# Forward substitution of a gated-DeltaNet kernel in its own lane, three rows in two steps

## The chip, the cores and the metric

The kernel runs on one core of one Trainium2 chip, in one launch. The metric is device time in microseconds (us), the median of three runs. The kernel before takes 1953.09 us (1953.03 to 1953.24). TensorE (PE) does the matmuls, VectorE (DVE) and ScalarE (ACT) work element by element, GpSimd (POOL) does a few selects and powers, and SyncE (SP) issues most DMAs. Each engine takes its instructions strictly in the order in which they stand in its own queue.

## The reference

One decoder block of width 2048 on 256 tokens, in float32: a half-step SwiGLU feed-forward, a mixer, a second feed-forward, a gated embedding, and a norm. The change is in the mixer, which projects the normed input by `W_in` into 14 blocks of 512 columns, runs a gated DeltaNet on 8 heads and a stick-breaking attention on 8 other heads, and projects both by `W_out`:

```
lmat = where(strict, einsum("bnhid,bnhjd->bnhij", k_beta, k) * decay, 0)     # 64 x 64 per chunk and head
sol  = triangular_solve(lmat + eye, rhs, lower, unit_diagonal)               # forward substitution
step: v_new = u - w S;  o = (q e^g) S + attn v_new;  S = S e^g_last + (k e^..)^T v_new
```

## The kernel before

**Steps.** Every large product is a loop over weight pairs. `accumulate` (L107 to L109) handles one pair of 256 weight rows by 512 columns in 12 matmuls of 512 columns. Float32 accuracy comes from splitting: `weight_pair` loads `raw` (SP, L69), casts it to `whi` on ACT (L72) and subtracts to get `wlo` on DVE (L73). PE uses `whi` in the first matmul of a pair and `wlo` in the second or third. I call one pair a step and number the steps of the mixer from 0: steps 0 to 111 are the 14 blocks of `W_in`, steps 112 to 143 are `W_out`. There are three buffers of `whi` and of `wlo`, so the split of pair n can start when step n-3 has ended.

**Lanes.** Beside the steps run generators in lanes. After each step `lanes.step()` advances the generator at the head of every lane to its next `yield`. So what a generator issues between two yields is spread over the steps. Lane CONV does the short convolutions, SYSTEM builds the triangular systems of a group of four heads (`system`, L940), CHAIN solves them and runs the recurrence (`chain`, L996), STICK runs the attention heads (`stick`).

**The solve.** The eight 128 x 128 systems of a head group (four heads, two halves of the tokens) are cut into 32 x 32 diagonal blocks, and all are inverted at once, row by row, for i from 1 to 31. Row i is one product (L1007, `pm`, 8(i+1) elements in each partition) and one reduction over it (L1009, into `sol`), both on DVE, and each needs the one before. Then `sol` goes to DRAM (L1013) and comes back turned into `Z` (L1017), DVE transposes three blocks of it into `X` (L1021 to L1023), and four small products join the blocks: t1 (L1029), z1 (L1037), t2 (L1047), z2 (L1053). Between them stand copies out of PSUM on ACT and DVE: `ts`, `X`, `Z`, `tw`. The recurrence follows: up, sp, op, ks, qs, vp, op (L1060), with `R` and others on DVE. `L`, the table of factors, has one buffer; the second group's `system` loads it (L988) once the first group's solve is done.

**Order.** The generators only fix in which order the instructions are recorded. A scheduler then orders each engine's queue by its own estimates, so a recorded instruction can go earlier than others that were recorded before it, if its inputs come earlier. `tc.keep_in_program_order` pins an instruction behind everything recorded so far on its engine.

Of the kernel before, what the change touches and what calls it, by code (L numbers as in the profile page):

```python
# [13 lines left out]
ALU = mybir.AluOpType  # L14
AX = mybir.AxisListType

P = 128
# [24 lines left out]
def block_kernel(ctx, tc, a, out):  # L42
    nc = tc.nc
# [11 lines left out]
    def mx_ps(name):  # L55
        return ps.tile([P, NB], F32, tag="mx", name=name, bufs=4)

    lanes = Lanes(4)
    dr = ctx.enter_context(tc.tile_pool(name="dr", bufs=1, space=bass.MemoryType.DRAM))


# [532 lines left out]
    def r1():  # L594
# [8 lines left out]

    stat = new_stat()
    nT = mixer(tc, nc, a, act, mm_ps, mx_ps, accumulate, picker, new_nT, norm_block, sumsq, block, lanes, transposed,
               nT, r, h, stat, ident, mhalf)
    r = rstd(stat)
# [94 lines left out]
def mixer(tc, nc, a, act, mm_ps, mx_ps, accumulate, picker, new_nT, norm_block, sumsq, block, lanes, transposed,  # L702
          nT, r, h, stat, ident, mhalf):
    xs = picker(*nT)
    C64 = P // 2
    CONV, CHAIN, STICK, SYSTEM = 0, 1, 2, 3
    blocks = list(W_IN_ORDER)

    with tc.tile_pool(name="mix", bufs=1) as mp, \
# [49 lines left out]
        def transpose4(name, src):  # L759
            tr = mx_ps(name)  # L760
            for c in range(4):
                nc.tensor.transpose(tr[:, c * P:(c + 1) * P], src(c), ident)
            return tr

        def bc(x):

            return x.rearrange("p (c o) -> p c o", o=1).broadcast_to([P, 4, P])

        def v3(x):
            return x.rearrange("p (c e) -> p c e", c=4)  # L770
# [4 lines left out]
        def w4(name, dt=F32):  # L775
            return mp.tile([P, 4 * T], dt, tag="w4", name=name, bufs=6)
# [87 lines left out]
        knq = [[mp.tile([P, 4, 2, P], F32, tag="kq", name="knq", bufs=4) for _ in range(2)] for _ in range(2)]  # L864
        kdec = [mp.tile([P, NB], F32, tag="kd", name="kdec", bufs=2) for _ in range(2)]
        vn_ = [w4("v").rearrange("p (t x) -> p t x", t=2) for _ in range(2)]
# [65 lines left out]
        def dn_block(part, hg):  # L932
            nat = to_sbuf(natural(2 * part + hg))
            lanes.add(CONV, conv_silu(nat, part, hg))


        o_nat = [mp.tile([P, 2, NB], F32, tag="onat", name="onat", bufs=2) for _ in range(2)]
# [3 lines left out]
        def system(hg):  # L941

            hs = slice(hg * 4, hg * 4 + 4)
            kq = knq[hg]
            while not decayed:
                yield

            dec = w4("dec").rearrange("p (t c i) -> p t c i", t=2, c=4)
            for t in range(2):
                gb = transpose4("gb", lambda c: gc[:, t, hg * 4 + c:hg * 4 + c + 1].broadcast_to([P, P]))  # L950
                for b, s in ((0, gc), (C64, sB)):
                    nc.vector.tensor_tensor(out=dec[:, t, :, b:b + C64], in0=v3(gb)[:, :, b:b + C64],
                                            in1=bc(s[:, t, hs])[:, :, 0:C64], op=ALU.subtract)
                nc.gpsimd.affine_select(out=dec[:, t], in_=dec[:, t], pattern=[[0, 4], [1, P]],
                                        compare_op=ALU.is_ge, fill=-1e30, base=0, channel_multiplier=-1)
                nc.scalar.activation(dec[:, t], dec[:, t], AF.Exp)
            yield
            yield
            while ready[hg] < 3:
                yield  # L960

            nc.vector.tensor_tensor(out=v3(kdec[hg]), in0=v3(kdec[hg]), in1=bc(eT[:, 0, hs]), op=ALU.mult)

            AT = w4("AT").rearrange("p (t c i) -> p t c i", t=2, c=4)
            for t in range(2):
                for pr in range(2):
                    kk = mx_ps("kk").rearrange("p (c w i) -> p c w i", c=2, w=2)
                    for q in range(2):
                        c = 2 * pr + q
                        nc.tensor.matmul(kk[:, q], kq[t][:, c, 0, :], kq[t][:, c], start=True, stop=True)  # L970
                    nc.vector.tensor_tensor(out=AT[:, t, 2 * pr:2 * pr + 2], in0=kk[:, :, 1, :],
                                            in1=dec[:, t, 2 * pr:2 * pr + 2], op=ALU.mult)
                    for q in range(2):
                        c = 2 * pr + q
                        nc.vector.scalar_tensor_tensor(out=dec[:, t, c], in0=kk[:, q, 0, :],
                                                       scalar=nbeta[:, t, hg * 4 + c:hg * 4 + c + 1], in1=dec[:, t, c],
                                                       op0=ALU.mult, op1=ALU.mult)
                yield
            N = dec.rearrange("p t c i -> p (t c) i")

            sc = dp.tile([H, 4, 32, 32], F32, tag="sc", name="sc", bufs=2)
            for b in range(4):
                nc.sync.dma_start(out=sc[:, b].rearrange("x j i -> j x i"),
                                  in_=N[32 * b:32 * b + 32, :, 32 * b:32 * b + 32])
            while hg and not solved[0]:
                yield
            L = mp.tile([P, 4 * T], F32, tag="lt", name="L")
            nc.sync.dma_start(out=L, in_=sc.rearrange("x b j i -> (x b) (j i)")  # L988
                              .rearrange("q (o n) -> q o n", o=1).broadcast_to([32, 4, 1024]))
            sol = mp.tile([P, 8, 32], F32, tag="sol", name="sol")  # L990
            nc.sync.dma_start(out=sol, in_=a["eye32"].rearrange("(o g) n -> o g n", o=1).broadcast_to([32, 4, 256]))
            for _ in range(5):
                yield
            systems[hg] = AT, N, L, sol

        def chain(hg):  # L996
            hs = slice(hg * 4, hg * 4 + 4)
            kq, v, o = knq[hg], vn_[hg], o_nat[hg]
            while hg not in systems:
                yield  # L1000
            AT, N, L, sol = systems[hg]

            nc.vector.memset(L[:, 0:1024:33], 1.0)
            Lv = L.rearrange("p (j i) -> p i j", j=32)
            for i in range(1, 32):
                pm = mp.tile([P, 8, 32], F32, tag="pm", name="pm")
                nc.vector.tensor_tensor(out=pm[:, :, 0:i + 1], in0=sol[:, :, 0:i + 1],  # L1007
                                        in1=Lv[:, i:i + 1, 0:i + 1].broadcast_to([P, 8, i + 1]), op=ALU.mult)
                nc.vector.tensor_reduce(out=sol[:, :, i:i + 1], in_=pm[:, :, 0:i + 1], axis=AX.X, op=ALU.add)  # L1009
                if i % 2:  # L1010
                    yield
            sc2 = dp.tile([H, 4, 32, 32], F32, tag="sc2", name="sc2", bufs=2)
            nc.sync.dma_start(out=sc2.rearrange("x b (g c) i -> (x b g) (c i)", g=4),  # L1013
                              in_=sol.rearrange("p c i -> p (c i)"))
            solved[hg] = True
            for b in range(4):
                nc.sync.dma_start(out=Z[32 * b:32 * b + 32, :, 32 * b:32 * b + 32],  # L1017
                                  in_=sc2[:, b].rearrange("x m i -> m x i"))
# [166 lines left out]
        def stick():  # L1185
            while not chain_done[0] or 1 not in systems:
                yield
            for part in range(2):
                sbT[part].append(mp.tile([P, 4, T], F32R, tag="kq", name="sbT", bufs=4))
            for part in range(2):  # L1190
                sbT[part].append(w4("sbT", F32R).rearrange("p (c x) -> p c x", c=4))
            live = {}
            for i in range(H + 3):
                if i >= 3:
                    stick_c(i - 3, live.pop(i - 3))
                if 2 <= i <= H + 1:
                    stick_b(live[i - 2])
                if i < H:
                    while sb_ready[i // 4] < 3:
                        yield  # L1200
                    live[i] = stick_a(i)
                yield
# [27 lines left out]
        for hg in range(2):  # L1230
            for part in (1, 0, 2):
                dn_block(part, hg)
            lanes.add(SYSTEM, system(hg))
            lanes.add(CHAIN, chain(hg))
        lanes.add(STICK, stick())
        for hg in range(2):
# [91 lines left out]
```

## Time and profile before

| | |
|---|---|
| median of three runs | 1953.09 us |
| profiled execution, its own time | 1952.66 us |
| its span, first to last instruction | 1950.9 us |
| busy in the span | PE 99%, DVE 82%, ACT 60%, POOL 7% |
| granted TensorE clock | 0.999 |

The mixer's steps 0 to 111 lie between 695 and 1068 us of the span. A step without anything else takes PE 2.72 us (12 matmuls, 0.227 us from one start to the next). The listed length of one matmul, 0.39 us, overlaps the next, so the distance of starts tells where PE lost time, and a bracket at a row's end tells the idle time before it and who ended it.

### The profile page before, as it was taken

Reading aid. Unit: us, or ns where it says so; the run is one execution under the profiler, and the core shown is the slowest. Engines: PE = TensorE matmul, PEld = TensorE weight load, DVE = VectorE, ACT = ScalarE, POOL = GpSimd, SP = SyncE. Lnnn points to the kernel's source line nnn. Section 1 sums busy time; section 2 is a strip of 40 time slices with the busy share of each in tenths; the row PEclk is TensorE's granted clock in tenths of the full one; section 3 lists DMA queues with packets and bytes.
Section 4 is the critical chain, followed back from the end, with each engine's and each line's share of the span. In section 5 each row is a group of like instructions: output and inputs, shape, how many; then the busy total and the mean of one; then the engine's idle time right before and its main releaser. Section 6 shows DMA issues by size and latency. Waiting matters only on the chain.

```text
span 1950.9 us, 24300 instructions
## 1 busy us (share of the span) xinstructions
PE 1930.9 (99%) x8888; PEld 1594.4 (82%) x8888; DVE 1591.7 (82%) x1737; ACT 1161.9 (60%) x1364; POOL 143.9 (7%) x220
## 2 busy tenths in 40 slices
PE   9999999999999999999999999999999999999998
PEld 7888888888888888878788888888888888888887
DVE  7879988998889766797856579889888998889765
ACT  7655666566665567664555456566565655656554
POOL 0010100000010000010100000010000100000000
PEclk9999999999999999999999999999999999999999
DMA  8778888888888765556564786788898987988764
GB/s 310 273 213 293 252 290 278 244 288 250 267 284 253 223 218 165 172 171 215 167 206 158 243 284 234 225 270 285 256 283 249 319 254 239 274 254 258 244 213 142
DMA packets 143895, 474.01 MB, mean 243 GB/s; under 512 B 19616, under 2 KB 47264, under 8 KB 129568
## 3 DMA queue, kind: packets, MB, share of 16 engines
q1 hardware_dynamic: 106048, 296.92, 43.7%
q0 software_dynamic: 25056, 157.30, 29.3%
q10 hardware_dynamic: 12672, 18.25, 3.1%
q8 instruction: 69, 1.13, 0.2%
q14 instruction: 50, 0.41, 0.1%
HBM read 450.39 MB, written 22.02 MB: 242 GB/s over the span
## 4 chain that ended last, share of the span: by engine, by line
PE 83%; DVE 9%; issue 5%; DMA 1%; ACT 1%; POOL 0%; SPq 0%; POOLq 0%; DVEq 0%; ACTq 0%
PE d L516 5%; PE d L518 5%; PE d L517 5%; PE u L517 5%; PE u L518 4%; PE u L516 4%; PE g L517 3%; PE g L518 3%; PE g L516 3%; PE g L326 3%; PE g L327 3%; PE g L325 3%; PE pj L108 3%; PE pj L109 3%; PE pj L107 3%
## 5 line engine op out<-in xcount | busy, mean ns | idle before, releaser
L72 ACT CAST whi<-raw 128x1024 fp32r<-128x1024 f32 (+1 forms) x493 | 515.8, 1050 | 424.1 <-PE pj L109 106.4
L73 DVE TENSOR_TENSOR wlo<-raw,whi 128x1024 fp32r<-128x1024 f32 (+1 forms) x493 | 595.9, 1216 | 160.9 <-ACT whi L72 160.0
L291 DVE TENSOR_TENSOR slo<-R,shi 128x2048 fp32r<-128x2048 f32 (+2 forms) x217 | 435.9, 2013 | 103.0 <-ACT shi L290 102.3
L290 ACT CAST shi<-R 128x2048 fp32r<-128x2048 f32 (+2 forms) x217 | 366.3, 1692 | 190.7 <-DVE R L295 76.4
L107 PE MATMUL pj<-whi,nTh 128*128 128x512 f32 x448 | 179.4, 401 | 0.0
L108 PE MATMUL pj<-wlo,nTh 128*128 128x512 f32 x448 | 175.4, 391 | 2.2 <-DVE wlo L73 2.2
L109 PE MATMUL pj<-whi,nTl 128*128 128x512 f32 x448 | 174.9, 390 | 0.0
L517 PE MATMUL d<-wlo,hTh 128*128 128x512 f32 x448 | 174.3, 389 | 0.0
L518 PE MATMUL d<-whi,hTl 128*128 128x512 f32 x448 | 174.0, 389 | 0.0
L516 PE MATMUL d<-whi,hTh 128*128 128x512 f32 x448 | 173.6, 390 | 0.0
L517 PE MATMUL u<-wlo,nTh 128*128 128x512 f32 x400 | 156.2, 390 | 3.4 <-DVE wlo L73 3.4
L517 PE MATMUL g<-wlo,nTh 128*128 128x512 f32 x400 | 156.0, 390 | 1.0 <-DVE wlo L73 1.0
L518 PE MATMUL g<-whi,nTl 128*128 128x512 f32 x400 | 155.9, 390 | 0.0
L518 PE MATMUL u<-whi,nTl 128*128 128x512 f32 x400 | 155.7, 389 | 0.0
L516 PE MATMUL g<-whi,nTh 128*128 128x512 f32 x400 | 155.1, 391 | 0.2 <-ACT whi L72 0.2
L516 PE MATMUL u<-whi,nTh 128*128 128x512 f32 x400 | 153.7, 389 | 0.0
L295 DVE TENSOR_TENSOR R<-R 128x2048 f32<-128x2048 f32 (+2 forms) x66 | 133.1, 2016 | 0.1
L108 PEld LDWEIGHTS pj<-wlo,nTh 128*128 128x128 f32 x448 | 84.2, 188 | 20.1 <-DVE wlo L73 4.1
L516 PEld LDWEIGHTS d<-whi,hTh 128*128 128x128 f32 x448 | 84.1, 188 | 17.9 <-ACT hTh L479 0.7
L518 PEld LDWEIGHTS d<-whi,hTl 128*128 128x128 f32 x448 | 84.1, 188 | 17.7
L109 PEld LDWEIGHTS pj<-whi,nTl 128*128 128x128 f32 x448 | 84.1, 188 | 17.6
L517 PEld LDWEIGHTS d<-wlo,hTh 128*128 128x128 f32 x448 | 84.1, 188 | 17.5
(311 smaller groups left out, 3472.8 us busy)
## 6 DMA issues: line engine op xcount, KB each, us to landing
raw<-in_w_gu SPq DMA_DIRECT2D x199, 512.0 KB, 5.7
raw<-in_w_down SPq DMA_DIRECT2D x112, 512.0 KB, 6.3
raw<-in_w_in SPq DMA_DIRECT2D x112, 512.0 KB, 3.4
R<-in_w_gu2q POOLq DMA_DIRECT2D x54, 1024.0 KB, 8.2
R<-in_w_gu1q POOLq DMA_DIRECT2D x48, 1024.0 KB, 8.5
raw<-in_w_out SPq DMA_DIRECT2D x32, 512.0 KB, 4.0
raw<-in_w_pg SPq DMA_DIRECT2D x32, 512.0 KB, 4.3
R<-in_w_down11q POOLq DMA_DIRECT2D x12, 768.0 KB, 6.2
```

The source lines that it names most:

```text
L72: nc.scalar.copy(hi[:, j, :], raw[:, j, :])
L73: nc.vector.tensor_tensor(out=lo[:, j, :], in0=raw[:, j, :], in1=hi[:, j, :], op=ALU.subtract)
L107: nc.tensor.matmul(outs[t], xh[:, c], whi[:, j, :], start=st, stop=False)
L108: nc.tensor.matmul(outs[t], xh[:, c], wlo[:, j, :], start=False, stop=False)
L109: nc.tensor.matmul(outs[t], xl[:, c], whi[:, j, :], start=False, stop=sp)
L290: nc.scalar.copy(hi, w)
L291: nc.vector.tensor_tensor(out=lo, in0=w, in1=hi, op=ALU.subtract)
L295: nc.vector.tensor_tensor(out=self.raw[x], in0=self.raw[x], in1=self.raw[y], op=ALU.add)
L325: nc.tensor.matmul(out, xh, whi[:, g, :], start=st, stop=False, skip_group_check=True)
L516: nc.tensor.matmul(out, xh[:, c], whi[:, j, :], start=st, stop=False, skip_group_check=True)
L517: nc.tensor.matmul(out, xh[:, c], wlo[:, j, :], start=False, stop=False, skip_group_check=True)
L518: nc.tensor.matmul(out, xl[:, c], whi[:, j, :], start=False, stop=sp, skip_group_check=True)
```

## The change

The loop over the rows is taken out of `chain` and becomes a generator of its own, `solve`, in a fifth lane, SOLVE. `chain` now waits until `solve` has stored its solution, and begins with the load of `Z`. So the solve of the second group no longer stands behind the recurrence of the first in one lane. A generator that yielded after every second row (`if i % 2`) now yields after two rows out of three (`if i % 3`). And the product of each row is pinned behind what was recorded for DVE before it.

```diff
-    lanes = Lanes(4)
+    lanes = Lanes(5)
...
-    CONV, CHAIN, STICK, SYSTEM = 0, 1, 2, 3
+    CONV, CHAIN, STICK, SYSTEM, SOLVE = range(5)
...
-        def chain(hg):
-            hs = slice(hg * 4, hg * 4 + 4)
-            kq, v, o = knq[hg], vn_[hg], o_nat[hg]
+        solutions = {}
+
+        def solve(hg):
             while hg not in systems:
                 yield
             AT, N, L, sol = systems[hg]
...
             for i in range(1, 32):
                 pm = mp.tile([P, 8, 32], F32, tag="pm", name="pm")
-                nc.vector.tensor_tensor(out=pm[:, :, 0:i + 1], in0=sol[:, :, 0:i + 1],
-                                        in1=Lv[:, i:i + 1, 0:i + 1].broadcast_to([P, 8, i + 1]), op=ALU.mult)
+                tc.keep_in_program_order(
+                    nc.vector.tensor_tensor(out=pm[:, :, 0:i + 1], in0=sol[:, :, 0:i + 1],
+                                            in1=Lv[:, i:i + 1, 0:i + 1].broadcast_to([P, 8, i + 1]), op=ALU.mult))
                 nc.vector.tensor_reduce(out=sol[:, :, i:i + 1], in_=pm[:, :, 0:i + 1], axis=AX.X, op=ALU.add)
-                if i % 2:
+                if i % 3:
                     yield
...
             solved[hg] = True
+            solutions[hg] = AT, N, sc2
+
+        def chain(hg):
+            hs = slice(hg * 4, hg * 4 + 4)
+            kq, v, o = knq[hg], vn_[hg], o_nat[hg]
+            while hg not in solutions:
+                yield
+            AT, N, sc2 = solutions[hg]
             for b in range(4):
...
             lanes.add(SYSTEM, system(hg))
+            lanes.add(SOLVE, solve(hg))
             lanes.add(CHAIN, chain(hg))
```

The rows below show what stands in the engines' queues. Of a product of eight elements in a row, `128x8x28` is row 27. The changed kernel's line numbers are 4 to 13 higher from L999 on.

ACT around the first head group's joining products, before (z1 stands before step 65 on PE, and the first cast after `ts` is that of step 66):

```order
L746 ACTIVATE nat<-pj,rstd_5474 128x512 x2
L1032 COPY ts<-t_7420 32x8x32
L72 CAST whi<-raw 128x1024 x2
L1040 COPY X<-z_7470 32x8x32
L1042 COPY Z<-z_7470 32x8x32
L72 CAST whi<-raw 128x1024 x2
L1054 COPY Z<-z_7551 64x8x64
```

Two casts stood between `ts` and `X`. The same place on ACT now (the casts ahead of `ts` end with that of step 69; the one behind `Z` is that of step 70):

```order
L746 ACTIVATE nat<-pj,rstd_5474 128x512 x2
L72 CAST whi<-raw 128x1024 x4
L1044 COPY ts<-t_7535 32x8x32
L1052 COPY X<-z_7579 32x8x32
L1054 COPY Z<-z_7579 32x8x32
L72 CAST whi<-raw 128x1024 x2
L1066 COPY Z<-z_7663 64x8x64
```

`X` and `Z` now follow `ts` at once, and four casts have gone ahead of all three. On PE now, from the end of z1 to the start of step 70 (before, the 12 matmuls of a step stood between z1, t2 and z2):

```order
L1051 MATMUL z_7579<-Z,ts 32x32
L1059 MATMUL t_7628<-X,dec 64x64 x8
L1065 MATMUL z_7663<-Z,tw 64x64 x7
L107 MATMUL pj<-whi,nTh 128x512 x2
L1065 MATMUL z_7663<-Z,tw 64x64
L108 MATMUL pj<-wlo,nTh 128x512
```

The three products now stand next to each other, just ahead of step 70.

DVE at that place, before (the `wlo` above `Z` is that of step 67):

```order
L73 TENSOR_TENSOR wlo<-raw,whi 128x1024
L1041 COPY Z<-z_7470 32x8x32
L1009 TENSOR_REDUCE sol<-pm 128x8
L1007 TENSOR_TENSOR pm<-sol,L 128x8x7
L1009 TENSOR_REDUCE sol<-pm 128x8
L1007 TENSOR_TENSOR pm<-sol,L 128x8x8
L1009 TENSOR_REDUCE sol<-pm 128x8
L1007 TENSOR_TENSOR pm<-sol,L 128x8x9
L1049 COPY tw<-t_7518 64x512
L1009 TENSOR_REDUCE sol<-pm 128x8
L73 TENSOR_TENSOR wlo<-raw,whi 128x1024
```

Eight instructions of rows and both copies stood between `wlo` 67 and `wlo` 68, and t1 to z2 lay three steps apart. Now (the first `wlo` is that of step 70):

```order
L1053 COPY Z<-z_7579 32x8x32
L1011 TENSOR_TENSOR pm<-sol,L 128x8x6
L1061 COPY tw<-t_7628 64x512
L1013 TENSOR_REDUCE sol<-pm 128x8
L1011 TENSOR_TENSOR pm<-sol,L 128x8x7
L1013 TENSOR_REDUCE sol<-pm 128x8
L1011 TENSOR_TENSOR pm<-sol,L 128x8x8
L73 TENSOR_TENSOR wlo<-raw,whi 128x1024
L1013 TENSOR_REDUCE sol<-pm 128x8
L73 TENSOR_TENSOR wlo<-raw,whi 128x1024 x3
```

Both copies now stand between `wlo` 69 and `wlo` 70, with two rows between `tw` and `wlo` 70.

DVE from `wlo` 80 on, before (the second group's solve ended ahead of `wlo` 75):

```order
L1183 TENSOR_TENSOR sbT<-so,sbT 128x256
L73 TENSOR_TENSOR wlo<-raw,whi 128x1024
L167 STREAM_TRANSPOSE tb<-nat 128x512 x2
L73 TENSOR_TENSOR wlo<-raw,whi 128x1024 x8
L167 STREAM_TRANSPOSE tb<-nat 128x512 x2
```

No row of a solve stood here. Now, from `wlo` 85 on (`wlo` 86 is the second):

```order
L73 TENSOR_TENSOR wlo<-raw,whi 128x1024
L1195 TENSOR_TENSOR sbT<-so,sbT 128x256
L1011 TENSOR_TENSOR pm<-sol,L 128x8x25
L1013 TENSOR_REDUCE sol<-pm 128x8
L1011 TENSOR_TENSOR pm<-sol,L 128x8x26
L1013 TENSOR_REDUCE sol<-pm 128x8
L1011 TENSOR_TENSOR pm<-sol,L 128x8x27
L1013 TENSOR_REDUCE sol<-pm 128x8
L73 TENSOR_TENSOR wlo<-raw,whi 128x1024
L1011 TENSOR_TENSOR pm<-sol,L 128x8x28
L1013 TENSOR_REDUCE sol<-pm 128x8
```

The second group's longest rows moved from steps 70 to 75 to steps 81 to 89. Over all, the first group's solve stands between `wlo` 39 and `wlo` 64 (before: 39 to 54) and the second's between `wlo` 66 and `wlo` 89 (before: 65 to 75). The order of all engines before step 40 and from step 112 on is the same as before.

## Rows read from the trace of the kernel before

**Rows 1.** Who PE waited for: total us, times, longest.
```profile
PE pj L108 <- DVE wlo L73: 2.2, 4, 1.1
PE vp L1060 <- DVE R L1081: 1.3, 1, 1.3
...
PE at L1172 <- DVE st L1165: 0.6, 1, 0.6
```

**Rows 2.** Stretches: length, PE, PEld, DVE, ACT, POOL busy, PE clock, DMA share, GB/s.
```profile
818.00:868.50 50.50, 49.37 (x239) 40.16 (x238) 46.66 (x101) 31.81 (x66) 5.86 (x4) 1.00 0.47 160
901.00:941.00 40.00, 38.74 (x282) 32.35 (x275) 38.16 (x87) 18.93 (x36) 0.53 (x1) 1.00 0.48 159
960.00:1060.00 100.00, 100.00 (x582) 83.98 (x581) 56.32 (x73) 52.89 (x84) 4.62 (x9) 1.00 0.59 190
```

**Rows 3.** PE in order of time: two waits, first matmuls of steps 76 and 80.
```profile
844.96 0.39 PE L107 MATMUL pj<-whi,nTh 128*128 128x512 f32 x1
845.65 0.50 PE L108 MATMUL pj<-wlo,nTh 128*128 128x512 f32 x1 [0.30 <-DVE wlo L73]
...
928.14 0.39 PE L109 MATMUL pj<-whi,nTl 128*128 128x512 f32 x1
929.79 1.13 PE L1060 MATMUL vp<-R,Z 128*128 128x128 f32 x8 [1.26 <-DVE R L1081]
...
948.51 0.58 PE L107 MATMUL pj<-whi,nTh 128*128 128x512 f32 x1
...
962.27 0.39 PE L107 MATMUL pj<-whi,nTh 128*128 128x512 f32 x1
```

**Rows 4.** A step without other work: DVE splits pair 93, PE uses it.
```profile
993.48 1.22 DVE L73 TENSOR_TENSOR wlo<-raw,whi 128x1024 fp32r<-128x1024 f32 x1 [1.50 <-ACT whi L72]
...
997.86 0.39 PE L108 MATMUL pj<-wlo,nTh 128*128 128x512 f32 x1
```

**Rows 5.** DVE in order of time around `tw`.
```profile
907.38 0.18 DVE L1009 TENSOR_REDUCE sol<-pm 128x8 f32<-128x48 f32 x1
907.59 0.25 DVE L1007 TENSOR_TENSOR pm<-sol,L 128x56 f32<-128x56 f32 x1
...
908.13 0.27 DVE L1007 TENSOR_TENSOR pm<-sol,L 128x64 f32<-128x64 f32 x1
...
909.01 0.69 DVE L1049 COPY tw<-t 64x512 f32<-64x512 f32 x1
909.74 0.23 DVE L1009 TENSOR_REDUCE sol<-pm 128x8 f32<-128x72 f32 x1
```

**Rows 6.** ACT and PE in order of time around z1 and t2.
```profile
905.35 0.36 ACT L1040 COPY X<-z 32x256 f32<-32x256 f32 x1
907.48 0.36 ACT L1042 COPY Z<-z 32x256 f32<-32x256 f32 x1 [1.76 <-DVE Z L1041]
...
907.75 1.14 PE L1047 MATMUL t<-X,dec 64*64 64x64 f32 x16
```

**Rows 7.** The second group's load of `L`, and who waits for it.
```profile
895.42 0.53 SPq L988 DMA_DIRECT2D L<-sc  x1
...
901.01 0.09 DVE L1003 MEMSET L<- 128x32 f32 x1 [0.70 <-DMA L<-sc]
...
901.33 0.71 DVE L167 STREAM_TRANSPOSE tb<-nat 128x512 f32<-128x512 f32 x1
```

**Rows 8.** Row 27 of both solves, by shape: total us, mean ns.
```profile
L1007 DVE TENSOR_TENSOR pm<-sol,L 128x224 f32<-128x224 f32 x2 | 1.1, 570 | 0.0
L1009 DVE TENSOR_REDUCE sol<-pm 128x8 f32<-128x224 f32 x2 | 0.8, 389 | 0.1
```

**Rows 9.** DVE on one stick-breaking head: two scans, two products, then the next.
```profile
948.77 0.99 DVE L1161 TENSOR_TENSOR_SCAN st<-st,one 128x128 f32<-128x128 f32 x2
949.68 0.96 DVE L1165 TENSOR_TENSOR st<-st 128x127 f32<-128x127 f32 x2
950.57 0.43 DVE L1021 STREAM_TRANSPOSE X<-Z 32x256 f32<-32x256 f32 x1
```

## The prediction

> **What bounds the kernel now.** I read the page first: PE is busy 99% of the span, DVE 82%. So nothing off PE shortens the kernel except by ending a wait of PE. The table of waits comes next, and it is short [rows 1]: in the mixer PE waits four times for `wlo`, once for `R` and once for a stick-breaking head. The longest of the four for `wlo`, 1.1 us, lies at 753 us, long before any solve, so the change leaves it alone. The stretches show why the others arise [rows 2]: during the two solves DVE is busy 46.7 of 50.5 us and 38.2 of 40.0 us, and in the 100 us from 960 on only 56.3. The split of a weight pair queues behind rows of the solve.
>
> PE's own order gives the size of such a wait better than the idle time does [rows 3]. Step 47's second matmul starts 0.69 us after its first, where 0.23 is normal: 0.46 lost. There are three such waits in the first solve (0.46, 0.64 and 0.51 by the same reading), together 1.6. At vp the start comes 1.65 after that of the matmul before, so 1.4 is lost. The head's wait is 0.6 [rows 1].
>
> How much delay a split can take: in an undisturbed step DVE starts pair 93 at 993.48, ends at 994.70, and PE wants it at 997.86 [rows 4]. A lead of 3.2 us is the most there is, because the cast waits for a buffer. DVE can be late by 3.2 before PE notices, and then PE pays all of the excess.
>
> **The change part by part.** No arithmetic goes or comes: 62 products, 62 reductions and every matmul stay. What changes is where they stand.
>
> *The first solve, spread over 24 steps instead of 14.* Row 27 costs 0.57 + 0.39 [rows 8] plus two handovers of 0.03 (the product at 907.59 starts 0.03 after the reduction's end [rows 5]), some 1.03 us; the shorter rows cost less. Two or three rows and a split of 1.22 fill more than a step of 2.72; one and a half rows leave room. DVE's queue now has at most two and a half rows between two splits up to `wlo` 64, and the crowded place, nine convolution products and two and a half rows between `wlo` 48 and 49, comes behind three nearly empty gaps, so the lead covers it. I take the 1.6 us as gained; bounds 0.8 (one of the three waits comes back in another place) and 1.6.
>
> *vp.* In the gaps behind the four splits ahead of it `R` now has rows 8 to 11 instead of rows 9 to 24, and the products before it give DVE steps of over 4 us. I take the 1.4 as gained; bounds 0.7 and 1.4. The head's wait stays: the same recurrence, the same power on POOL and again three rows stand between op and the first head. Bounds -0.6 and +0.9, taken as 0.
>
> *The knot ahead of step 70.* Here the change adds waits. z1, t2 and z2 now follow each other on PE, and what joins them is on ACT and DVE: `X`, then t2, then `tw`, then z2. Behind `tw` DVE still has the reduction of row 5, row 6 and the product of row 7 before `wlo` 70, and on ACT the cast of pair 70 is behind `X` and `Z`. So everything of step 70 is queued behind a chain that starts only when z1 ends. A handover is 0.12 (t2 ends at 908.89, `tw` starts at 909.01 [rows 5, 6]). From the end of z1: 0.12 + 0.36 (`X`) + 0.12 + 1.14 (t2 [rows 6]) + 0.12 = 1.86 to the start of `tw`; 0.73 to the next reduction, 0.75 from there to a product two instructions on, 0.19 for that one [rows 5], 1.22 for the split and 0.12 to PE: 4.87. In that time PE has t2, z2 (as long as t2) and two first matmuls, 2.73. It loses 2.1. Below, if DVE were free: `tw` 0.69, z2 and the same two matmuls behind 1.86 give 4.26 with a handover, a loss of 1.5. Above, if DVE is a row late when z1 ends: 3.1. I take 2.1, all of whose pieces stand in rows. `Z` on ACT waits for DVE's `Z` [rows 6], but that path with the cast takes about 2.1 and is not last.
>
> *The late rows of the second solve.* The rows are recorded at one and a half a step, so the longest, 24 to 31, come between `wlo` 85 and `wlo` 89. DVE has there four splits at 1.13 from start to start (1.22 less an overlap of 0.09, as 949.68 against 948.77 + 0.99 [rows 9]) and eight rows of about 1.03, together 12.7, with one short product left out; PE needs 4 x 2.72 = 10.9. The excess is 1.8 unless DVE comes with a lead. It comes with almost none: from `wlo` 81 to 85 it has four splits (4.5), four heads at 1.8 (950.57 - 948.77 [rows 9]), two transposes at 0.62 (0.71 less the overlap [rows 7]) and six rows of some 0.75 (they are shorter, and the heads between them fill the handovers), in all 17.4. PE's steps with the same heads took 962.27 - 948.51 = 13.8 before [rows 3]. That eats 3.6, a little more than the 3.2 there can be. So the loss is 1.8 + 0.4 = 2.2, which I take; nothing if both sums are 15% too high, 5.4 if DVE has no lead at `wlo` 81.
>
> *The reload of `L`.* It is issued when the first solve's last row is done, and the pinned rows make DVE's `memset` of `L` wait for it, with two transposes, a block of `X` and `wlo` 66 behind. It lands 5.6 us after its issue (895.42 to 901.01 [rows 7]); then 0.1 + 0.7 + 0.7 + 0.4 + 1.2 to the end of `wlo` 66, and 0.5 for issuing the store ahead of it: 9.2. The last row, just behind `wlo` 63, ends between 2.5 before and 0.7 after the start of step 63 (a lead of 3.2 or none), and PE wants `wlo` 66 at 3 x 2.72 + 0.23 = 8.4 after that start. So the loss is 0 to 1.5; I take 0.2, since little stands ahead of `wlo` 62 and 63.
>
> *Sum.* -1.6 - 1.4 + 2.1 + 2.2 + 0.2 = +1.5. The profiled execution took 1952.66, so it would take 1954.2. The median of the runs is 0.43 above that execution, which makes 1954.6.
>
> [...] On DVE an instruction that does not need the one before starts about 0.08 before its end (949.68 against 949.76 [rows 9]); one that does starts 0.03 after. So a row mixed with convolutions costs less than one by itself, and the pinned order mixes more. [...]
>
> **The rivals.**
> *The new waits hide.* If the knot costs only its lower 1.5 and the late rows nothing, the sum is -1.6 - 1.4 + 1.5 = -1.5, time 1951.6; with nothing at the knot either -3.0, 1950.1. For it: DVE has 44 us to spare in the 100 behind the solves [rows 2]. Against it: order, not sum, decides there. Even all waits of the mixer that the change can touch, 1.6 + 1.4 + 0.6, give 3.6.
> *DVE's backlog from step 79 to step 89 decides, and the kernel is slower.* The scaling of `onat` and the wait for a power on POOL stand just ahead of the heads, now with rows 15 to 17 between. If they bring DVE to `wlo` 81 without its lead of 3.2, PE pays those 3.2 too, and the wait of the first head grows by up to 0.9. The sum becomes +5.6, time 1958.7. It decides from about 2.4 us of missing lead on, where +1.5 becomes +3.9. For it: 17.4 against 13.8 with the heads at full length. Against it: PE's steps ahead of the heads, with the recurrence's products, are long, and each wait of PE gives DVE its lead back.
> *Mixing gives nothing.* Some 30 instructions between `wlo` 48 and `wlo` 84 stand mixed; at 0.11 each (0.08 + 0.03) that is 3.3 more of DVE work, of which the lead of the first solve takes about 1. Time 1954.6 + 2.3 = 1956.9. Against it stands the row itself.
> *The change does nothing.* The solve leaves the first group's lane, but if DVE only trades waits one for one, the time stays at 1953.1, +-0.5. It lies inside the forecast's own range.
>
> **How the numbers follow.** A difference under 0.2% (3.9 us) is what a measurement of this kernel can't tell from none. Forecast (with the trade one for one) 0.58, own range 1952.0 to 1957.2; new waits hide 0.16; backlog 0.20; mixing gives nothing 0.06. Faster by over 0.2% means under 1949.2, which needs more than every wait I could find: 0.05, a third of the first rival. Slower means above 1957.0: all of the backlog, 0.20, and 0.03 from the ends of the others, 0.23. Within: 0.72. The range leaves out the lower end of the first rival and the upper end of the second: 1950.5 to 1959.0.
>
> **What would show it.** Right: the waits for `wlo` in the first solve and the wait of vp gone from the table; a pause at z2 and at the second or third matmul of step 70 that ends with DVE, together about 2 us; two or three waits for `wlo` in steps 84 to 88, 2 us together; the granted clock unchanged at 1.00. Wrong: a wait of PE for `wlo` between steps 40 and 64 over 0.5 us (then DVE is not relieved); no pause at step 70 (then the copies don't hang on z1 as I read it); DVE idle between steps 81 and 89 (then the backlog is not there); or a wait for `L` that ends on PE at step 66 with over 1 us.

## The result, and the profile after

The changed kernel takes 1956.07 us (1955.15 to 1957.67, 21 runs) against 1953.24 us of the kernel before in the same runs: ratio 1.0014, 95% interval 1.0008 to 1.0020. It is slower by 2.8 us. The interval excludes a ratio of 1, though the loss lies inside the 0.2% that I took as the limit of what can be told. The prediction was 1954.6 with a range of 1950.5 to 1959.0. The profiled execution has a span of 1953.5 us, 2.6 more than before. Of these, 0.4 lie ahead of step 0, whose first matmul starts at 695.28 where it started at 694.87. The order of all engines is the same there, so that part is not the change, and the mixer has to account for 2.2.

The table of PE's waits, of the stretch from 690 to 1075 us of the changed kernel (columns as in [rows 1]):

```profile
PE pj L108 <- DVE wlo L73: 2.5, 3, 1.3
PE z L1065 <- ACT whi L72: 0.8, 1, 0.8
PE t L1059 <- ACT X L1052: 0.5, 1, 0.5
PE at L1184 <- DVE st L1177: 0.4, 1, 0.4
...
```

The wait for `R` is gone, and two waits are new, at t2 and z2. The table's three waits for `wlo` are not those of before. The longest lies at 980 us, 1.1 is the old one at 754 us, and the third is at 1060 us. None is left in the first solve. The stretches of [rows 2] say why:

```profile
818.00:868.50 50.50, 50.50 (x249) 42.30 (x248) 38.42 (x82) 33.07 (x67) 4.77 (x4) 1.00 0.51 169
901.00:941.00 40.00, 38.58 (x279) 31.94 (x278) 22.66 (x43) 18.00 (x28) 0.00 (x0) 0.96 0.65 212
...
960.00:1060.00 100.00, 98.16 (x576) 81.07 (x574) 72.25 (x127) 51.55 (x87) 7.41 (x14) 1.00 0.56 174
```

In the first solve DVE is busy 38.4 us where it was 46.7, and PE is busy without a gap. In the third stretch DVE has 72.3 where it had 56.3, and PE loses 1.8. In the second, DVE is nearly half idle and PE still loses 1.4, and the granted clock is 0.96 there. That is the place ahead of step 70. PE in order of time there (start, length; a bracket is the idle time and who ended it):

```profile
917.02 0.19 PE L1051 MATMUL z<-Z,ts 32*32 32x32 f32 x1
917.68 1.14 PE L1059 MATMUL t<-X,dec 64*64 64x64 f32 x16 [0.47 <-ACT X L1052]
919.66 0.99 PE L1065 MATMUL z<-Z,tw 64*64 64x64 f32 x14 [0.83 <-ACT whi L72]
920.58 0.73 PE L107 MATMUL pj<-whi,nTh 128*128 128x512 f32 x2
921.24 0.47 PE L1065 MATMUL z<-Z,tw 64*64 64x64 f32 x2
921.83 0.80 PE L108 MATMUL pj<-wlo,nTh 128*128 128x512 f32 x1
922.42 0.63 PE L109 MATMUL pj<-whi,nTl 128*128 128x512 f32 x1
922.85 0.63 PE L108 MATMUL pj<-wlo,nTh 128*128 128x512 f32 x1
...
924.82 0.40 PE L107 MATMUL pj<-whi,nTh 128*128 128x512 f32 x1
```

By the distance of starts, less what is usual for such a pair, t2 comes 0.65 late, z2 0.99 and the third matmul of step 70 comes 0.37 late: 2.0 in all. Then comes something that I had not forecast. From 921.83 to 924.82 seven matmuls take 2.99 where seven times 0.227 is 1.59. Most stand 0.43 apart, and nothing is waited for. The stretches of the same place show the granted clock (the column ahead of the last two):

```profile
920.60:921.20 0.60, 0.60 (x3) 0.28 (x2) 0.60 (x2) 0.00 (x0) 0.00 (x0) 1.00 0.00 0
921.20:921.80 0.60, 0.51 (x3) 0.28 (x2) 0.60 (x2) 0.05 (x1) 0.00 (x0) 0.50 0.00 0
...
924.00:924.50 0.50, 0.50 (x2) 0.36 (x2) 0.50 (x1) 0.00 (x0) 0.00 (x0) 0.50 0.99 295
```

The clock is at its lower level (1.2 of 2.4 GHz) from 921.2 to 924.5 and at 1.00 again from 924.8, behind two pauses with small products between them. That costs 1.4. ACT and DVE in order of time show what step 70 waited for:

```profile
917.27 0.36 ACT L1052 COPY X<-z 32x256 f32<-32x256 f32 x1 [5.48 <-PE z L1051]
917.66 0.41 DVE L1053 COPY Z<-z 32x256 f32<-32x256 f32 x1 [4.24 <-ACT X L1052]
...
918.11 0.36 ACT L1054 COPY Z<-z 32x256 f32<-32x256 f32 x1 [0.48 <-DVE Z L1053]
918.50 1.99 ACT L72 CAST whi<-raw 128x1024 fp32r<-128x1024 f32 x2
918.86 0.69 DVE L1061 COPY tw<-t 64x512 f32<-64x512 f32 x1 [0.64 <-PE t L1059]
...
920.55 1.22 DVE L73 TENSOR_TENSOR wlo<-raw,whi 128x1024 fp32r<-128x1024 f32 x1
```

ACT is idle 5.48 us ahead of `X`, with the cast of pair 70 behind it in the queue. That cast, the first of the two at 918.50, ends at 919.55, and so does `tw` on DVE. The bracket at z2 names the cast, but z2 reads `tw`, so this trace alone does not tell which of the two held PE. The other new loss is at step 86. Here are DVE and PE in order of time, three rows of the solve between two splits:

```profile
974.81 1.22 DVE L73 TENSOR_TENSOR wlo<-raw,whi 128x1024 fp32r<-128x1024 f32 x1
...
978.83 0.38 DVE L1013 TENSOR_REDUCE sol<-pm 128x8 f32<-128x216 f32 x1
979.13 1.22 DVE L73 TENSOR_TENSOR wlo<-raw,whi 128x1024 fp32r<-128x1024 f32 x1
980.26 0.55 DVE L1011 TENSOR_TENSOR pm<-sol,L 128x224 f32<-128x224 f32 x1
```

```profile
978.71 0.39 PE L107 MATMUL pj<-whi,nTh 128*128 128x512 f32 x1
980.40 0.50 PE L108 MATMUL pj<-wlo,nTh 128*128 128x512 f32 x1 [1.30 <-DVE wlo L73]
...
983.02 0.39 PE L107 MATMUL pj<-whi,nTh 128*128 128x512 f32 x1
```

The matmul at 980.40 starts 1.69 after the one before it, so 1.46 is lost there. The whole step, from 978.71 to the first matmul of the next at 983.02, takes 4.31 where 2.72 is normal, because the next start comes 0.1 late as well. Steps 85 and 87 are 0.2 and 0.35 longer than normal, so the late rows cost 2.2. And vp, which lost 1.4 before [rows 3], now follows without a gap:

```profile
943.40 0.40 PE L109 MATMUL pj<-whi,nTl 128*128 128x512 f32 x1
943.63 1.05 PE L1072 MATMUL vp<-R,Z 128*128 128x128 f32 x8
```

### The profile page after: what moved, and what is told of

The parts are those of the page before. It is cut to its first block, busy times and chain, and to the rows that moved or that the text cites. A ratio compares the mean times of both kernels' runs of the same rounds, so it can differ in the third digit from the quotient of the medians.

```text
span 1953.5 us, 24303 instructions
## 1 busy us (share of the span) xinstructions
PE 1932.8 (99%) x8888; PEld 1595.9 (82%) x8888; DVE 1587.6 (81%) x1737; ACT 1162.3 (59%) x1364; POOL 142.6 (7%) x220
## 4 chain that ended last, share of the span: by engine, by line
PE 85%; DVE 8%; issue 5%; ACT 1%; DMA 1%; POOL 0%; SPq 0%; POOLq 0%; ACTq 0%; DVEq 0%
PE d L516 5%; PE d L517 5%; PE d L518 5%; PE u L517 5%; PE u L518 4%; PE u L516 4%; PE pj L108 4%; PE pj L109 3%; PE g L517 3%; PE pj L107 3%; PE g L518 3%; PE g L516 3%; PE g L327 3%; PE g L326 3%; PE g L325 3%
```

## The experiments

Each is timed against the kernel before on one chip. The theory to begin with (theory 1): the pin makes the gain and the loss, and the loss is three products next to each other ahead of step 70, plus the late rows.

**The products kept apart.** Edit on the changed kernel (e1):

```diff
-                nc.tensor.matmul(t2[64:128, x, :], N[0:64, x, 64:128], X[0:64, x, :], start=True, stop=True)
+                tc.keep_in_program_order(
+                    nc.tensor.matmul(t2[64:128, x, :], N[0:64, x, 64:128], X[0:64, x, :], start=True, stop=True))
```

> The changed kernel with the matmuls of t2 kept in program order on PE, so that z1, t2 and z2 stand three steps apart (70, 71, 72) and nothing else of the solve moves. Theory 1 (the three contiguous products cost the pauses of 0.65 and 0.99 us and 0.25 at the third matmul of step 70, and the low clock behind them another 1.5): all four go, 3.4 us less than the changed kernel, 1952.7 us, granted clock 1.00 from 915 to 930. Rival A (DVE and ACT still do the same copies and rows between the splits, so the wait only moves to steps 71 to 73): 1955.5 to 1956. Rival B (the low clock at 921 us has nothing to do with the pauses): the pauses go, the low clock stays somewhere near, 1954.2.

Measured 1957.32 us, ratio 1.0020 (1.0011 to 1.0029). Theory 1 falls on this point. PE in order of time, from the end of z1:

```profile
916.89 0.19 PE L1051 MATMUL z<-Z,ts 32*32 32x32 f32 x1
919.46 1.22 PE L107 MATMUL pj<-whi,nTh 128*128 128x512 f32 x2 [2.38 <-ACT whi L72]
```

The pauses joined into one of 2.55, which ends with the cast of pair 70, and the low clock stayed, here from 919.2 to 926.0. Next to each other, t2 and z2 had filled part of that pause with work that has to be done anyway. Rival A was right that the wait only moves, though not to the steps it named.

**Only z2 moved.** The same edit at z2 instead of t2 (e2).

> The changed kernel with only the matmuls of z2 kept in program order: z1 and t2 stay together ahead of step 70, z2 goes two steps on. Theory 1 (the clock falls when pauses and the small products follow each other for some 4 us): the pause for X, 0.65, stays; the 0.99 for tw goes; the wait for the split of pair 70 grows to about 0.7, because two rows and tw stand ahead of it on DVE; clock 1.00; 1956.07 - 0.99 - 1.5 + 0.5 = 1954.1. Rival (a pause of 0.65 with small products around it is enough for the low clock): 1.5 more, 1955.6, granted clock under 0.7 for some us after the pause.

Measured 1957.44, ratio 1.0022 (1.0013 to 1.0030); both forecasts missed. PE in order of time:

```profile
920.49 1.22 PE L107 MATMUL pj<-whi,nTh 128*128 128x512 f32 x2 [0.77 <-ACT whi L72]
922.73 0.80 PE L108 MATMUL pj<-wlo,nTh 128*128 128x512 f32 x1 [1.02 <-DVE wlo L73]
```

The pause at z2 became one for the cast, and the split behind it, which DVE does after `tw` and rows, is later still. The low clock came here too, from 920.4 to 927.2, though z2 no longer stands there. In both runs a pause ends with the cast of pair 70, and in e1 DVE itself is idle for 1.1 us ahead of the split, waiting for that cast. This suggests ACT as the seat: theory 2.

**No pin.** The changed kernel with the plain product again (e3):

```diff
-                tc.keep_in_program_order(
-                    nc.vector.tensor_tensor(out=pm[:, :, 0:i + 1], in0=sol[:, :, 0:i + 1],
-                                            in1=Lv[:, i:i + 1, 0:i + 1].broadcast_to([P, 8, i + 1]), op=ALU.mult))
+                nc.vector.tensor_tensor(out=pm[:, :, 0:i + 1], in0=sol[:, :, 0:i + 1],
+                                        in1=Lv[:, i:i + 1, 0:i + 1].broadcast_to([P, 8, i + 1]), op=ALU.mult)
```

> The changed kernel without the pin: own lane and two yields in three rows, the product of a row goes as early as the scheduler wants. Theory 1 (the pin alone makes both the gain and the loss): the first solve's rows stand as before, three waits for wlo, 1.6 us, come back; vp has at most half of its 1.4 left; no knot at step 70, no rows behind wlo 77, no low clock: 1952 to 1953.5, the kernel before within 1 us. Rival (the lane and the slower yields make the loss): pauses at the joining products or at steps 84 to 88 stay, 1955 to 1956.

Measured 1952.32, ratio 0.9994 (0.9985 to 1.0002), as theory 1 had it. One of the three old waits of the first solve, by PE in order of time:

```profile
850.09 0.50 PE L108 MATMUL pj<-wlo,nTh 128*128 128x512 f32 x1 [0.43 <-DVE wlo L73]
```

Steps 47 to 52 are 2.2 us longer than without these waits, as before. No pause stands at step 70 and none at step 86. The wait of vp does not come back: the table of waits has none for `R`, and a new one of 0.4 at sp.

**Pin only.** The pin in the kernel before, with its lanes and its `if i % 2` (e4; the same lines the other way round).

> The kernel before with the pin alone: solve in the chain, every second row a yield. Theory 1 (the pin decides): the first solve's waits for wlo and that for R go (3.0 us), z1, t2 and z2 are again next to each other, ahead of step 65, with pauses of 1 to 2 us and a low clock of 1 to 1.5 behind them, and the second solve's rows, two a step to wlo 94, cost 0 to 1.5: 1952.5 to 1955. Rival (without its own lane the solve gains nothing, or the yields of two in three are what relieves DVE): waits for wlo of over 1 us in all stay between 830 and 890 us.

Measured 1952.15, ratio 0.9993 (0.9984 to 1.0002), a little under what theory 1 said. The products stand nearly together, with two large matmuls between t2 and z2; the pauses are short there (0.64, 0.34 and 0.37 by the distance of starts) and the clock stays at 1.00:

```profile
904.80 1.14 PE L1049 MATMUL t<-X,dec 64*64 64x64 f32 x16 [0.47 <-ACT X L1042]
...
906.77 0.99 PE L1055 MATMUL z<-Z,tw 64*64 64x64 f32 x14 [0.17 <-issue]
907.98 0.50 PE L108 MATMUL pj<-wlo,nTh 128*128 128x512 f32 x1 [0.21 <-DVE wlo L73]
```

But the rival's mark is there too: of the waits for `wlo`, one of three new ones,

```profile
879.57 0.50 PE L108 MATMUL pj<-wlo,nTh 128*128 128x512 f32 x1 [0.67 <-DVE wlo L73]
```

The three make steps 56 to 58 longer by 2.1. With two rows a step the pin only moves the first solve's waits from 846 to 863 us to behind 872 us. It takes the slower yields to end them.

**`X` behind the casts.** Edit on the changed kernel (e5):

```diff
-            nc.scalar.copy(X[32:64, :, 0:32], z1[32:64, :, 0:32])
+            tc.keep_in_program_order(nc.scalar.copy(X[32:64, :, 0:32], z1[32:64, :, 0:32]))
```

> The changed kernel with the first copy of z1 (`X`, ACT) pinned behind the casts recorded before it, so that the casts of pairs 70 and 71 stand ahead of `X` and `Z` on ACT. Theory 2 (the loss at step 70 sits on ACT: the cast of pair 70 waits behind two copies that need z1, which stands just ahead of step 70 on PE; which product follows which on PE matters little): no pause over 0.5 us between 905 and 930 us, granted clock 1.00 there, 3.5 us less than the changed kernel: 1952.6. Rival A (DVE is the seat, with rows 3 to 5 ahead of the split of pair 70): a wait for wlo of 0.5 to 2 us stays at step 70, 1953 to 1955. Rival B (the low clock comes from elsewhere): the pauses go, the clock stays low for some us, 1954.

Measured 1952.62, ratio 0.9996 (0.9987 to 1.0005): theory 2. ACT in order of time (the two casts are those of pairs 70 and 71), and the stretch:

```profile
914.43 1.05 ACT L72 CAST whi<-raw 128x1024 fp32r<-128x1024 f32 x1 [2.22 <-DMA raw<-in_w_in]
915.70 1.06 ACT L72 CAST whi<-raw 128x1024 fp32r<-128x1024 f32 x1 [0.22 <-DMA raw<-in_w_in]
917.69 0.37 ACT L1052 COPY X<-z 32x256 f32<-32x256 f32 x1 [0.94 <-PE z L1051]
```

```profile
905.00:930.00 25.00, 25.00 (x209) 20.17 (x208) 14.80 (x28) 12.28 (x15) 0.00 (x0) 1.00 0.74 252
```

The weights of pair 70 landed at 914.4, three microseconds before z1 ended. The cast could run, and only its place in the queue had kept it. PE has no gap in 25 us and the clock is 1.00.

The edit moves more than `X`. The scheduler also set t2 and z2 a step apart, so that PE's order is that of e1, matmul for matmul. What e5 has other than e1 is ACT's order, `X` and `Z` behind the cast of pair 70, and with it DVE's, where two splits now stand ahead of the copy `Z`. This order is worth 4.7 us (1957.32 to 1952.62), and products set apart without it gained nothing. The same order with the three products next to each other was not run.

**Rows spread evenly.** On top of e5 (e6):

```diff
-                if i % 3:
+                if i % (2 if hg and i < 16 else 3) or hg and i > 18:
```

> As e5_x_behind_casts, and the second group's rows spread otherwise: two yields in three up to row 15 become one in two (the short rows go together into the long steps 73 to 77), and from row 19 on each row has a step of its own. Theory 2 (the wait of 1.5 us at step 86 comes from three and two long rows between two splits): it goes, 1.6 us less than e5: 1951.0, 2.2 us under the kernel before. Rival (the stick-breaking heads of steps 81 to 85 use up DVE's lead whatever the rows do): the wait moves to steps 82 to 85, e5 within 0.5 us.

Measured 1950.05, ratio 0.9981 (0.9973 to 0.9990). Waits of PE from 690 to 1180 us:

```profile
PE pj L108 <- DVE wlo L73: 1.1, 1, 1.1
PE at L1184 <- DVE st L1177: 0.6, 1, 0.6
...
```

The only wait for `wlo` left in the mixer is the old one at 754 us. Steps 85 to 87 take 8.3 us where e5 has 10.1, and step 108 takes 2.72 where e5 has 3.17. Over all 112 steps the trace gives 2.0; the medians differ by 2.6, and their intervals are too wide to say what the rest is. This version beats both kernels: 3.5 us under the kernel before, and some 6 under the changed one.

**A pause between full matmuls.** On top of e5, one long reduction ahead of the split of pair 90 (e7):

```diff
+            if hg:
+                tc.keep_in_program_order(nc.vector.tensor_reduce(
+                    out=pm[:, 0, 0:4], in_=L.rearrange("p (o n) -> p o n", o=1).broadcast_to([P, 4, 1024]), axis=AX.X, op=ALU.add))
             solved[hg] = True
```

> As e5_x_behind_casts, with one extra reduction on DVE behind the second solve's last row (four times over `L`, its result not used), some 4.4 us, ahead of the split of pair 90. PE has to pause about 2.3 us at step 90, between full matmuls of 512 columns on both sides. If a pause of that length is enough for the low clock: matmuls 0.43 us apart for some 3 us behind it, granted clock near 0.5, and the time is e5 + 2.3 + 1.5. If the small products around the pause at step 70 were needed as well: clock 1.00 behind it, e5 + 2.3.

Measured 1956.72, 4.1 above e5, ratio 1.0017 (1.0008 to 1.0025). PE in order of time:

```profile
988.27 0.39 PE L107 MATMUL pj<-whi,nTh 128*128 128x512 f32 x1
990.95 0.79 PE L108 MATMUL pj<-wlo,nTh 128*128 128x512 f32 x1 [2.30 <-DVE wlo L73]
...
994.40 0.40 PE L107 MATMUL pj<-whi,nTh 128*128 128x512 f32 x1
```

The pause is 2.46 by the starts, and eight intervals take 3.45 behind it where 1.82 is normal: 1.6 more. So a pause between full matmuls brings the low clock by itself; small products are not needed. What e7 does not settle is how the two pauses of 0.65 and 0.99 with t2 between them come to count as one.

**No lane.** The kernel before with the pin and with `if i % 3`, the solve inside the chain (e8).

> The kernel before with pin and slower yields, but the solve left inside the chain. Theory 2 (the lane only sets where the second group's chain stands): the first solve's waits for wlo are gone as in the changed kernel, z1, t2 and z2 stand at step 70 again with the low clock, and the second group's recurrence lies at steps 109 to 117, inside W_out, which needs its output at step 118: a new wait of PE there of 3 us or more, so 1959 or above. Rival (the lane changes nothing that counts, since the second group's solve has room enough): 1956, as the changed kernel.

Measured 1969.89, ratio 1.0081 (1.0067 to 1.0095). The stretch at `W_out`:

```profile
1085.00:1120.00 35.00, 26.27 (x82) 18.53 (x82) 14.12 (x25) 8.49 (x16) 1.64 (x1) 0.80 0.36 119
```

PE is idle for 8.7 of 35 us, at a mean clock of 0.80. The first solve's waits are gone here too, so the relief comes from pin and yields. The lane keeps the second group's recurrence out of `W_out`, once the yields are slower.

The joining products bring the low clock here, as forecast. PE in order of time, and two stretches:

```profile
921.93 1.14 PE L1049 MATMUL t<-X,dec 64*64 64x64 f32 x16 [0.45 <-ACT X L1042]
...
923.91 0.99 PE L1055 MATMUL z<-Z,tw 64*64 64x64 f32 x14 [0.17 <-issue]
925.12 0.79 PE L108 MATMUL pj<-wlo,nTh 128*128 128x512 f32 x1 [0.21 <-DVE wlo L73]
```

```profile
921.00:925.00 4.00, 3.28 (x76) 2.56 (x65) 2.27 (x4) 3.41 (x5) 0.00 (x0) 1.00 0.02 4
925.00:928.40 3.40, 3.28 (x8) 2.60 (x9) 2.34 (x3) 0.36 (x1) 0.00 (x0) 0.51 0.64 199
```

These are the pauses of e4, within 0.02 us, and there the clock stayed at 1.00. So the length of the pauses alone does not decide whether it falls.

## Why the prediction was right or wrong

The time and its sign came out, 1.5 us above the forecast of 1954.6 and inside its own range of 1952.0 to 1957.2. That it came so close is in part luck, since the terms below miss in both directions. A wait also delays the matmul behind the one that waits, so I measure by whole steps, from the first matmul of a step to that of the next. In the kernel before, step 47, whose wait stands in [rows 3], ends here:

```profile
848.28 0.39 PE L107 MATMUL pj<-whi,nTh 128*128 128x512 f32 x1
```

It took 3.32 from 844.96, so 0.60 was lost where the prediction read 0.46. Term by term, in us:

| term | predicted | measured |
|---|---|---|
| waits for `wlo` in the first solve (steps 47 to 52) | -1.6 | -2.2 |
| vp | -1.4 | -1.5 |
| stick-breaking head | 0 | -0.2 |
| pauses at step 70 and the low clock behind them | +2.1 | +2.9 |
| late rows (steps 85 to 87) | +2.2 | +2.2 |
| reload of `L` | +0.2 | 0 |
| elsewhere (above all steps 57 and 108) | none | +1.0 |
| sum | +1.5 | +2.2 |

The 112 steps take 375.6 us where they took 373.4, which is the sum. Of what lies elsewhere, 0.4 is at a transposition that waits for ACT (878.49 us); it is in each timed kernel that has lane, pin and slower yields, and not in e3, e4 and e8. Another 0.45 is in step 108, where the split of its pair is late (1060.06 us), and e6 does without it.

*The two gains* came, that of the first solve with 0.6 more than the upper bound of 1.6: each wait also cost the next matmul 0.1, and step 50 lost another 0.2 that was not counted. For this gain e3 and e4 show that pin and slower yields are both needed: without the pin the waits return in their old place, with two rows a step they return behind 872 us. The wait of vp is gone in e3, without the pin, and in e4, without the slower yields, so neither of them is needed for that gain.

*The knot* was right in size and in path. The pauses are 2.0 by the distance of starts, and from the end of z1 (917.21) to the third matmul of step 70 (921.83) it is 4.62 where the forecast had 4.87. The step "everything of step 70 is queued behind a chain that starts only when z1 ends" holds. But what I put first, that the three products stand next to each other, was no cost that setting them apart could save (e1). What saves it is to take `X` and `Z` from ahead of the cast of pair 70 (e5 against e1). I had written of the path through `Z` and the cast that it "takes about 2.1 and is not last". In the changed kernel the cast ends together with `tw`, at 919.55, so that path took 2.3 and is as late as the one through `tw`, but not later. With the low clock, steps 69 to 72 take 18.1 us where e5 has 15.1, less than 2.0 and 1.4 together: in e5, t2 and z2 each lengthen a step by 1.3, while here the sixteen matmuls of t2 take 1.0.

*The granted clock* is what the prediction had wrong. It gave the clock as unchanged at 1.00, without a term or a reason. It fell to 0.50 for 3.3 us and cost 1.4, the largest term that the forecast lacked. The larger gain in the first solve made up for part of it.

*The late rows* were right: 2.2, in steps 85 to 87. DVE's split of pair 81 ends 3.0 us before PE uses it, and those of pairs 85 to 87 end 0.1 before, so the lead is used up where the prediction had it used up. e6 shows that the loss goes when the rows are spread.

*The reload of `L`* cost PE nothing: DVE's splits of pairs 66, 67 and 68 end 1.2, 0.7 and 1.2 us before PE uses them. The cast of pair 68 waited for its weights, not for the table.

*The rivals.* New waits hiding: wrong, they cost 5.1 with the clock. DVE's backlog of +5.6: wrong, DVE had 3.0 of its 3.2 us of lead at `wlo` 81. Mixing gives nothing: wrong, DVE still starts an instruction that needs nothing from the one before ahead of its end (980.26 against 979.13 + 1.22 = 980.35), and the first solve's waits went. The Trainium skill, VectorE: DVE Perf Modes, section The DRAIN you can't avoid, has the next instruction wait for an empty pipe, and adds that a next one that is not held starts earlier; these rows agree with the addition. The change does nothing: wrong, the interval of the ratio excludes 1.

## What to carry to other kernels

An instruction that waits for late input holds up everything behind it on its engine, so when a change moves work, look at what stands directly behind each moved copy, above all casts and splits that feed the busiest engine. Where that engine is matmul-bound, price a pause of some 2.5 us at 1.6 to 2.2 times its length (2.5 + 1.6 in e7, 2.55 + 3.1 in e1), since the clock fell behind it. A chain that is taken out of a lane can be spread to one row a step, and its gain counts only when its last rows don't meet other work.

## What the runs showed of the hardware

The granted clock of TensorE went to its lower level behind pauses between matmuls of 2.46 us (e7) and 2.55 us (e1), and behind two of 0.65 and 0.99 us with small products between them (the changed kernel). It stayed at 1.00 behind one of 1.46 us (step 86). Behind 0.64, 0.34 and 0.37 us in a row it stayed at 1.00 in e4, and behind nearly the same pauses it fell to the lower level in e8. Executions of one kernel differ as well. Of e4's eleven, two have a mean clock of 0.996 and the others 0.998 or 0.999, and these two are the longest (1953.42 and 1953.78 us). Of e1's eleven, one has 0.999, and it is the shortest (1955.94 us). So the length of the pauses is not all that decides, and what else does stays open. In the changed kernel and in e7 the lower level lasted some 3 us and cost 1.4 and 1.6. In e1, with its one pause, it lasted 6.8 us and cost 3.1: steps 69 to 72 take 20.8 us there and 15.1 in e5, which has the same order on PE, and 2.55 of that is the pause.

DVE starts an instruction that needs nothing from the one before some 0.09 us before that one's listed end (980.26 against 980.35), as in the kernel before [rows 9].
